# A long fused layer on one core: the closing V chunk in plain fp32, eight more gathered rows beside it, and the list work dealt anew

## The chip, the cores and the metric

One core of a Trainium2 chip runs the whole kernel in one launch. The metric is the device time of one execution in microseconds (us), as the median of the runs. The profile and the trace are of one further execution.

## The reference, cut to what matters

The kernel computes one layer of a hybrid network on 256 tokens of width 2048: retention and a gated linear recurrence side by side, cross attention, and then a layer of single-neuron experts, which is where the change lies. Everything is float32.

```python
def peer_ffn(xn, w_q, sub_keys, u_tab, v_tab):
    ...                                      # scores over 2 x 128 sub-keys, 8 heads
    eid = (i1 * PEER_N_KEYS + i2)...         # 8 x 16 of 16384 experts for each token
    gate = jax.nn.softmax(top_sc, axis=-1)...
    def block(args):
        xb, eb, gb = args
        u = u_tab[eb]
        act = jax.nn.gelu(jnp.einsum('td,tkd->tk', xb, u))
        return jnp.einsum('tk,tkd->td', gb * act, v_tab[eb])
```

For each token, 128 experts are chosen; each adds gate * gelu(u . x) * v to the token's row. A final RMSNorm over the row follows.

## The kernel before, in words

**Two ways to an expert.** The 16384 experts lie in 128 groups of 128. Some groups are done for all tokens as dense matrix products: 40 fixed ones (chunks 0 to 4 of eight groups each, tables U and V in a layout of their own) and 32 that are picked at run time as the fullest (chunks 5 to 8, whose columns are gathered by indirect DMA from the tables Us and Vs). What is left of each token's choices is done row by row: this is the *list*. For each half of the tokens (tt 0 and 1; 128 tokens lie on the 128 partitions) and each of 38 slots k (BASE), one indirect DMA gathers a row of Us for every token (128 rows of 8 KB), a *dot* (line 1438, VectorE) multiplies it with x and sums; later one gathers the row of Vs and an *axpy* (line 1446, VectorE) adds it, scaled, to the result hh. Two more gathers, the *spill*, hold what did not fit; their rows enter by TensorE (lines 1643, 1665).

**Stages.** `steps` is a list of steps made by `u_steps` and `v_steps` and run by `run`. First come the U products of chunks 5 to 8 (64 steps: a gathered column is transposed on TensorE, split and multiplied). Then come the V products in the order of ORDER: chunks 0, 1, 2, 3, 5, 6, 7, 8, with 16 steps each, into eight PSUM tiles `acc`. The ninth, chunk 4, is the closing one and is written out in `v_final`.

**Two forms of a V step.** A rounded step splits its table tile into `hi` (a cast to fp32r, ScalarE, line 1364) and `lo` (the rest, VectorE, line 1383) and its activations likewise, and issues three fp32r products: hi with both activation parts, lo with the first (lines 1175 to 1178 in `v_mms`, 1188 to 1191 in `r_mms`). A plain step, for the chunks named in PLAIN (5 and 7), multiplies the float32 tile as it stands (line 1197 in `p_mms`), with no hi and lo. The activations of a chunk that is not plain are split by `rounded` and `left` (lines 1307 and 1311), attached to the steps of the chunk before.

**Who deals the list.** The list is a generator, `chosen`. After each step, `run` calls `wv.pump(step.rate)`: it adds the step's rate to a credit and lets the list run while there is credit; a list item costs 2.2. The rates are RU for U steps on gathered columns, RV for rounded V steps, RP for plain ones. Each item first issues the gathers for which a buffer of `ring` is free (on POOL's queue, line 1431), then its own dot or axpy. All instructions of an engine run in the order written; so a rate decides how many dots, axpys and gathers stand between two steps on VectorE and POOL. What is left when the steps have run out is drained.

**The closing chunk.** END takes the last list axpys out of the list; `ending` deals them out one to a tile of the closing chunk, with three buffers in turn. Between the steps and the closing chunk stands a branch that is not taken with these data (line 1556, `rest`, more rows for tokens that overflow); every engine passes it. `v_final` loads its 16 V tiles on SP's queue (line 126) into four raw buffers, splits each (`high`, `low`), and multiplies it by `v_mms`. Tiles of output quarter 3 are kept split and come last, once for each tt, so that the first half of the tokens can be normed and written while the second is multiplied.

```python
RG, RK, RU, RV, RP = 8.0, 3.5, 1.9, 1.25, 3.1
PLAIN = (5, 7)
END = 4
ORDER = (0, 1, 2, 3, 5, 6, 7, 8, 4)
```

## Time and profile before

| | us |
|---|---|
| median of 3 runs | 2041.74 (2039.88 to 2043.61) |
| the profiled execution, its own time | 2037.77 |
| its span | 2036.0 |
| TensorE busy (a busy TensorE is not one at its peak) | 1895.3 |
| VectorE busy | 1539.9 |
| ScalarE busy | 882.8 |
| POOL busy | 520.8 |

Times of the trace are microseconds from the span's start. The U steps on gathered columns run from about 1278 to 1508 us, V chunks 0 to 3 to 1723, chunk 5 (plain) and chunk 6 to 1848, chunk 7 (plain) and chunk 8 to 1976, the closing chunk and the norm to 2036. PE stands for TensorE, PEld for its weight loads, DVE for VectorE, ACT for ScalarE, SP for SyncE. One plain float32 matmul leaves two MATMUL records in the trace.

### The profile page before, as it was taken

How to read it: one execution, taken by the hardware profiler on the slowest of the kernel's cores; microseconds unless marked ns; L12 is line 12 of the kernel's file. 1: busy time of each engine (PE TensorE's matmuls, PEld its weight loads, DVE VectorE, ACT ScalarE, POOL GpSimd, SP SyncE). 2: the span in 40 equal slices, each digit the busy share in tenths (PEclk: the TensorE clock that was granted, in tenths of full speed). 3: DMA queues.
4: the chain of work that ended last, by engine and by line, in shares of the span. 5: the costliest groups of instructions: out<-in, count | busy, mean ns of one | idle time of the engine just before them, and what ended most of it. 6: DMA issues, size and time to landing. Idle time of an engine off the chain costs nothing.

```text
span 2036.0 us, 27487 instructions
## 1 busy us (share of the span) xinstructions
PE 1895.3 (93%) x10068; PEld 1574.0 (77%) x10068; DVE 1539.9 (76%) x2366; ACT 882.8 (43%) x1382; POOL 520.8 (26%) x371
## 2 busy tenths in 40 slices
PE   9999999999999999999889778999998998969698
PEld 8888888888889888888788667899886776455376
DVE  6868967754566557999967666999797987776866
ACT  6556444544555555554456523333343432020143
POOL 1200010000000000000055410555434566765621
PEclk9999999999999999999999889999999998989899
DMA  8775656566555467556458685998989899989963
GB/s 293 264 219 171 200 177 197 160 191 192 186 176 156 145 185 288 169 178 201 155 131 172 160 274 183 394 385 291 381 320 410 290 348 378 366 310 398 362 241 123
DMA packets 203244, 499.86 MB, mean 246 GB/s; under 512 B 106760, under 2 KB 113032, under 8 KB 174856
## 3 DMA queue, kind: packets, MB, share of 16 engines
q1 hardware_dynamic: 72288, 254.23, 38.1%
q0 software_dynamic: 36240, 228.29, 29.1%
q10 hardware_dynamic: 94576, 15.54, 4.4%
q8 instruction: 79, 1.29, 0.3%
q14 instruction: 61, 0.50, 0.1%
HBM read 503.24 MB, written 21.30 MB: 258 GB/s over the span
## 4 chain that ended last, share of the span: by engine, by line
PE 51%; DMA 15%; issue 12%; DVE 12%; POOL 6%; ACT 2%; ACTq 1%; POOLq 0%; SPq 0%; DVEq 0%
PE wb L143 10%; PE xc L186 6%; PE xc L185 6%; PE xc L188 6%; PE wb L145 5%; DMA at<-in_Us_dram,idx 4%; DMA at<-in_Vs_dram,idx 3%; DVE lo L134 3%; POOL at L1431 3%; PE U L143 3%; PE U L145 1%; DMA h<-in_Vs_dram,idx 1%; PE G L1127 1%; DMA gt<-gs 1%; PE acc L1178 1%
## 5 line engine op out<-in xcount | busy, mean ns | idle before, releaser
L134 DVE TENSOR_TENSOR lo<-raw,hi 128x1024 fp32r<-128x1024 f32 x364 | 448.9, 1235 | 207.3 <-PE xc L188 125.6
L133 ACT CAST hi<-raw 128x1024 fp32r<-128x1024 f32 x364 | 381.7, 1051 | 290.0 <-PE xc L186 175.2
L143 PE MATMUL U<-xn,hi 128*128 128x512 f32 x1152 | 310.9, 406 | 0.0
L143 PEld LDWEIGHTS U<-xn,hi 128*128 128x128 f32 x1152 | 211.6, 194 | 36.1 <-ACT hi L133 0.2
L1438 DVE SCALAR_TENSOR_TENSOR junk<-at,h 128x2048 bf16<-128x2048 f32 x71 | 162.3, 2286 | 19.3 <-DMA at<-in_Us_dram,idx 19.3
L145 PEld LDWEIGHTS U<-xn,lo 128*128 128x128 f32 x1152 | 157.6, 192 | 23.6 <-DVE lo L134 12.7
L145 PE MATMUL U<-xn,lo 128*128 128x256 f32 x1152 | 163.2, 285 | 9.7 <-DVE lo L134 9.7
L1446 DVE SCALAR_TENSOR_TENSOR hh<-at,coef,hh 128x2048 f32<-128x2048 f32 x54 | 127.0, 2351 | 45.4 <-DMA at<-in_Vs_dram,idx 43.8
L1364 ACT CAST hi<-kept 128x1024 fp32r<-128x1024 f32 x52 | 53.6, 1050 | 220.5 <-DMA kept<-in_Vs_dram,dyn 138.2
L781 POOL DMA_DIRECT2D hn<-h x2 | 1.1, 564 | 509.6 <-DVE h L779 509.6
L1431 POOL DMA_INDIRECT at<-in_Us_dram,idx x71 | 83.9, 1181 | 132.4 <-DVE junk L1438 100.9
L143 PE MATMUL wb<-hT,hi 128*128 128x512 f32 x448 | 116.9, 397 | 0.0
L1197 PE MATMUL acc<-kept,kept 128*128 128x512 f32 x256 | 111.0, 594 | 3.0 <-DMA kept<-in_Vs_dram,dyn 3.0
L1431 POOL DMA_INDIRECT at<-in_Vs_dram,idx x54 | 100.1, 1854 | 48.9 <-DVE hh L1446 26.9
L1114 POOL TENSOR_TENSOR kept<-kept 128x512 f32<-128x512 bf16 x64 | 77.7, 1222 | 122.3 <-DVE kept L1113 89.3
L1175 PE MATMUL acc<-hi,xe 128*128 128x512 f32 x240 | 97.4, 406 | 6.6 <-ACT hi L1364 6.6
L1197 PEld LDWEIGHTS acc<-kept,kept 128*128 128x128 f32 x256 | 48.5, 190 | 64.4 <-issue 58.5
L1176 PE MATMUL acc<-hi,xe 128*128 128x512 f32 x240 | 95.9, 400 | 0.0
L1113 DVE TENSOR_TENSOR kept<-kept,kept 128x512 bf16<-128x512 bf16 x128 | 70.0, 595 | 28.4 <-POOL kept L1114 17.3
L143 PEld LDWEIGHTS wb<-hT,hi 128*128 128x128 f32 x448 | 80.7, 189 | 13.9
L1127 PE MATMUL G<-kept,kept 128*128 128x128 f32 x512 | 73.8, 296 | 18.6 <-POOL kept L1114 10.2
L143 PE MATMUL wb<-xT,hi 128*128 128x512 f32 x352 | 89.8, 397 | 0.0
(500 smaller groups left out, 4150.2 us busy)
## 6 DMA issues: line engine op xcount, KB each, us to landing
raw<-in_U_dram SPq DMA_DIRECT2D x80, 512.0 KB, 4.0
raw<-in_V_dram SPq DMA_DIRECT2D x60, 512.0 KB, 6.4
raw<-in_w_qkv_dram SPq DMA_DIRECT2D x48, 512.0 KB, 3.6
raw<-in_w_xyg_dram SPq DMA_DIRECT2D x44, 512.0 KB, 4.3
raw<-in_w_xk_dram SPq DMA_DIRECT2D x32, 512.0 KB, 3.5
raw<-in_w_xv_dram SPq DMA_DIRECT2D x32, 512.0 KB, 3.6
raw<-in_w_out_dram SPq DMA_DIRECT2D x32, 512.0 KB, 3.5
raw<-in_w_xq_dram SPq DMA_DIRECT2D x32, 512.0 KB, 3.5
```

The lines of the kernel that those rows point to most:

```text
L133: A.copy(hi, raw)
L134: V.tensor_tensor(lo, raw, hi.bitcast(F32), op=ALU.subtract)
L143: PE.matmul(pt, hi[:, ks], xt[:, kb, :], start=(kb == 0), stop=(kb == KB - 1))
L145: PE.matmul(pt[:, :T], lo[:, ks], xt[:, kb, :T], start=False, stop=False)
L185: PE.matmul(pt, xh, hi[:, w], start=(n == 0 and k == 0), stop=False)
L186: PE.matmul(pt, xl, hi[:, w], start=False, stop=False)
L188: PE.matmul(pt, xh, lo[:, w], start=False, stop=(n == 7 and k == 1))
L1175: PE.matmul(pt, ah[:, c, t_], hi[:, w], start=(first and c == 0), stop=False)
L1197: PE.matmul(acc[dc][tt], av[:, c, tt * P:(tt + 1) * P], row[:, dc * 512:(dc + 1) * 512], start=False, stop=False)
L1431: G.indirect_dma_start(dst, None, src, bass.IndirectOffsetOnAxis(ap=ix, axis=0), bounds_check=n - 1, oob_is_err=False)
L1438: V.scalar_tensor_tensor(junk, gat, 1.0, h[0], op0=ALU.mult, op1=ALU.mult, accum_out=coef[tt][:, k:k + 1])
L1446: V.scalar_tensor_tensor(hh[tt], gat, coef[tt][:, k:k + 1], hh[tt], op0=ALU.mult, op1=ALU.add)
```

## The change

Three edits go together.

1. Chunk 4 joins PLAIN. It is the closing one, so `v_steps` still makes no plain steps for it (a chunk under NCH keeps its form), but its activations are no longer split, and `v_final` multiplies float32 tiles as they are loaded: no `high`, no `low`, four plain matmuls a tile in place of twelve fp32r ones. Its tiles go into the buffers of raw, hi and lo in turn, eleven in all, ten loaded ahead.
2. END goes from 4 to 12: eight more axpys leave the list for the closing chunk. `ending` uses all free buffers, five, in place of three.
3. The rates are set anew: RU 1.9 to 2.05, RV 1.25 to 1.2, RP 3.1 to 2.0.

`dot` takes a first slot k0, which matters only behind the branch.

```diff
-RG, RK, RU, RV, RP = 8.0, 3.5, 1.9, 1.25, 3.1
-PLAIN = (5, 7)
-END = 4
+RG, RK, RU, RV, RP = 8.0, 3.5, 2.05, 1.2, 2.0
+PLAIN = (4, 5, 7)
+END = 12
...
-        if i in PLAIN:
+        if i in PLAIN and i >= NCH:
...
     def ending():
         free = ring + [h[0]]
+        deep = len(free) - 1
         held = []
-        for m in range(len(closing) + 3):
-            if m >= 3:
-                _, tt, k, _ = closing[m - 3]
-                axpy(tt, k, held[m - 3])
+        for m in range(len(closing) + deep):
             if m < len(closing):
                 _, tt, k, _ = closing[m]
-                held.append(fetch(free[m % 3], a["Vs"], NS, idx[tt][:, k:k + 1]))
-            if m >= 2:
+                held.append(fetch(free[m % len(free)], a["Vs"], NS, idx[tt][:, k:k + 1]))
+            if m >= deep:
+                _, tt, k, _ = closing[m - deep]
+                axpy(tt, k, held[m - deep])
                 yield
...
         def load(t):
             if t < len(tiles):
                 dc, q = tiles[t]
-                raws[t] = raw_tile(a["V"][i, dc, q])
+                tag, n = (("raw", 4), ("hi", 4), ("lo", 3))[(0, 1, 0, 1, 2, 0, 1, 2, 0, 1, 2)[t % 11]]
+                raws[t] = ws.tile([P, 1024], F32, tag=tag, name="last", bufs=n)
+                nc.sync.dma_start(raws[t], a["V"][i, dc, q])
...
+        def products(t, tts):
+            dc, q = tiles[t]
+            for tt in tts:
+                for k in range(2):
+                    c = 2 * q + k
+                    PE.matmul(acc[dc][tt], av[:, c, tt * P:(tt + 1) * P], raws[t][:, k * 512:(k + 1) * 512],
+                              start=False, stop=False)
...
-                v_mms(ah, al, his[t], los[t], q, list(enumerate(acc[dc])))
+                products(t, range(TT))
...
-                if t in (0, 2) or t > 2:
-                    next(last_rows, None)
+                next(last_rows, None)
...
-                v_mms(ah, al, vl[q][:, 0], vl[q][:, 1], q, [(tt, pt)])
+                products(12 + q, (tt,))
```

The list's rows (dots, spill dots and axpys on VectorE), counted in the two written orders: U stage 54 before and 58 now; V chunks 0 to 3 together 37 and 36; chunk 5 21 and 14; chunk 6 10 and 9; chunk 7 21 and 14; chunk 8 7 and 11; closing 4 and 12.

Gathers on POOL's queue in chunk 7. L1263 is a column of the chunk, 1 MB for two steps; L1431 a row of the list, 1 MB too; the names are the buffers. Before:

```order
L1263 DMA kept_7753<-in_Vs_dram,dyn 128x2048
L1431 DMA at_10570<-in_Vs_dram,idx 128x2048
L1431 DMA at_10566<-in_Vs_dram,idx 128x2048
L1263 DMA kept_7747<-in_Vs_dram,dyn 128x2048
L1431 DMA h_4236<-in_Vs_dram,idx 128x2048
L1431 DMA at_10568<-in_Vs_dram,idx 128x2048
L1431 DMA at_10570<-in_Vs_dram,idx 128x2048
L1263 DMA kept_7748<-in_Vs_dram,dyn 128x2048
L1431 DMA at_10566<-in_Vs_dram,idx 128x2048
L1431 DMA h_4236<-in_Vs_dram,idx 128x2048
L1431 DMA at_10568<-in_Vs_dram,idx 128x2048
L1263 DMA kept_7752<-in_Vs_dram,dyn 128x2048
```

Now:

```order
L1263 DMA kept_7753<-in_Vs_dram,dyn 128x2048
L1431 DMA at_10568<-in_Vs_dram,idx 128x2048
L1431 DMA h_4236<-in_Vs_dram,idx 128x2048
L1263 DMA kept_7747<-in_Vs_dram,dyn 128x2048
L1431 DMA at_10570<-in_Vs_dram,idx 128x2048
L1431 DMA at_10566<-in_Vs_dram,idx 128x2048
L1263 DMA kept_7748<-in_Vs_dram,dyn 128x2048
L1431 DMA at_10568<-in_Vs_dram,idx 128x2048
L1431 DMA h_4236<-in_Vs_dram,idx 128x2048
L1263 DMA kept_7752<-in_Vs_dram,dyn 128x2048
```

Where three list rows stood between two columns for most of the chunk, there are two now.

VectorE at the end of chunk 8, up to the branch (L1555 loads its condition). L1383 is a lo of chunk 8, L1446 an axpy, L1288 a gate of chunk 4, L1524 and L1528 the weights of the spill. Before:

```order
L1446 SCALAR_TENSOR_TENSOR hh_14527<-at_10568,coef,hh_14527 128x2048
L1288 TENSOR_TENSOR kept_7755<-raw,kept_7755 128x8x128
L1383 TENSOR_TENSOR lo<-kept_7747,hi 128x1024
L1446 SCALAR_TENSOR_TENSOR hh_14527<-kept_7749,coef,hh_14527 128x2048
L1383 TENSOR_TENSOR lo<-kept_7747,hi 128x1024
L1383 TENSOR_TENSOR lo<-kept_7752,hi 128x1024 x2
L1524 TENSOR_TENSOR od<-od,spg 128x2
L1528 TENSOR_SCALAR oh<-iota,spt,od 128x128 x2
L1383 TENSOR_TENSOR lo<-kept_7748,hi 128x1024
L1555 TENSOR_LOAD many
L1556 COMPARE_AND_BRANCH
```

Now:

```order
L1383 TENSOR_TENSOR lo<-kept_7748,hi 128x1024
L1383 TENSOR_TENSOR lo<-kept_7751,hi 128x1024
L1446 SCALAR_TENSOR_TENSOR hh_14543<-at_10570,coef,hh_14543 128x2048
L1383 TENSOR_TENSOR lo<-kept_7751,hi 128x1024
L1383 TENSOR_TENSOR lo<-kept_7754,hi 128x1024
L1446 SCALAR_TENSOR_TENSOR hh_14543<-at_10566,coef,hh_14543 128x2048
L1383 TENSOR_TENSOR lo<-kept_7754,hi 128x1024
L1446 SCALAR_TENSOR_TENSOR hh_14543<-at_10568,coef,hh_14543 128x2048
L1446 SCALAR_TENSOR_TENSOR hh_14543<-h_4236,coef,hh_14543 128x2048
L1555 TENSOR_LOAD many
L1556 COMPARE_AND_BRANCH
```

Before, the list ended in the middle of chunk 8 and the branch stood ahead of the last five lo's; now list rows are dealt up to the last lo and two stand behind it, and the branch stands behind these.

VectorE in the closing chunk as it is now, behind the branch. L1619 adds a finished output quarter:

```order
L1556 UNCONDITIONAL_BRANCH x2
L1446 SCALAR_TENSOR_TENSOR hh_14543<-at_10568,coef,hh_14543 128x2048
L1446 SCALAR_TENSOR_TENSOR hh_14543<-h_4236,coef,hh_14543 128x2048
L1446 SCALAR_TENSOR_TENSOR hh_14543<-kept_7749,coef,hh_14543 128x2048
L1446 SCALAR_TENSOR_TENSOR hh_14543<-kept_7750,coef,hh_14543 128x2048
L1446 SCALAR_TENSOR_TENSOR hh_14543<-h_4235,coef,hh_14543 128x2048
L1619 TENSOR_TENSOR hh_14542<-hh_14542,acc_14196 128x512
```

Five axpys from five buffers stand ahead of the first quarter's sum; before, the 16 lo's of the closing chunk stood here with four axpys among them.

## Rows read from the trace of the kernel before

**Rows 1.** The page's head and its part 1: busy us (share of the span) and instructions of TensorE.

```profile
span 2036.0 us, 27487 instructions
PE 1895.3 (93%) x10068; PEld 1574.0 (77%) x10068; DVE 1539.9 (76%) x2366; ACT 882.8 (43%) x1382; POOL 520.8 (26%) x371
```

**Rows 2.** Busy time by stage: the stretch and its us, then busy us and instructions of PE, PEld, DVE, ACT and POOL, the granted clock, the DMA share, GB/s of recorded packets.

```profile
1278.00:1508.00 230.00, 225.32 (x1447) 202.01 (x1447) 204.73 (x267) 85.73 (x186) 112.13 (x83) 0.99 0.92 351
1508.00:1723.00 215.00, 187.54 (x771) 149.10 (x770) 179.71 (x149) 72.88 (x76) 122.70 (x75) 0.94 0.94 359
1723.00:1848.00 125.00, 105.90 (x321) 62.99 (x320) 93.13 (x49) 18.30 (x18) 89.89 (x50) 0.93 0.90 344
1848.00:1976.00 128.00, 105.74 (x322) 64.28 (x321) 91.51 (x54) 26.15 (x27) 67.41 (x40) 0.91 0.87 335
1976.00:2036.00 60.00, 50.85 (x210) 38.97 (x208) 36.79 (x48) 21.59 (x34) 9.67 (x7) 0.95 0.39 134
```

**Rows 3.** What TensorE waited for from 1508 to 1976 us: us in total, times, the longest.

```profile
PE acc L1191 <- DVE lo L1383: 33.5, 9, 15.5
PE acc L1178 <- DVE lo L1383: 19.4, 9, 9.2
```

**Rows 4.** What VectorE waited for from 1640 to 1950 us, the longest in total.

```profile
DVE hh L1446 <- DMA at<-in_Vs_dram,idx: 43.8, 23, 7.7
```

**Rows 5.** DMA issues from 1278 to 1425 us (U stage): number, median us from issue to landing. All gathers of 1.05 MB.

```profile
at<-in_Us_dram,idx POOLq DMA_INDIRECT x34, 8.6
row<-in_Us_dram,dyn POOLq DMA_INDIRECT x14, 9.4
h<-in_Us_dram,dyn POOLq DMA_INDIRECT x7, 9.7
at<-in_Us_dram,spi POOLq DMA_INDIRECT x1, 6.2
```

**Rows 6.** The same from 1723 to 1930 us (chunks 5, 6, 7 and the start of 8), with the line on recorded packets.

```profile
DMA packets 11283, 74.06 MB, mean 358 GB/s; under 512 B 2247, under 2 KB 2247, under 8 KB 2247
...
at<-in_Vs_dram,idx POOLq DMA_INDIRECT x39, 9.4
kept<-in_Vs_dram,dyn POOLq DMA_INDIRECT x26, 8.8
h<-in_Vs_dram,idx POOLq DMA_INDIRECT x14, 9.6
```

**Rows 7.** The same over the whole U stage, 1278 to 1508 us. Where a size stands (KB each), it is that; the rest are gathers of 1.05 MB.

```profile
h<-hn POOLq DMA_DIRECT2D x1, 1024.0 KB, 7.6
at<-in_Us_dram,idx POOLq DMA_INDIRECT x51, 8.2
raw<-in_V_dram SPq DMA_DIRECT2D x1, 512.0 KB, 3.9
row<-in_Us_dram,dyn POOLq DMA_INDIRECT x18, 9.5
h<-in_Us_dram,dyn POOLq DMA_INDIRECT x9, 9.7
at<-in_Us_dram,spi POOLq DMA_INDIRECT x2, 8.3
at<-hn,spti POOLq DMA_INDIRECT x2, 7.6
```

**Rows 8.** The same over chunks 5 to 8, 1723 to 1976 us.

```profile
raw<-in_V_dram SPq DMA_DIRECT2D x6, 512.0 KB, 6.8
fg<-in_fg_dram SPq DMA_DIRECT2D x1, 1024.0 KB, 7.5
at<-in_Vs_dram,idx POOLq DMA_INDIRECT x41, 9.3
kept<-in_Vs_dram,dyn POOLq DMA_INDIRECT x29, 8.8
h<-in_Vs_dram,idx POOLq DMA_INDIRECT x15, 9.6
kept<-in_Vs_dram,idx POOLq DMA_INDIRECT x2, 7.1
at<-in_Vs_dram,spi POOLq DMA_INDIRECT x2, 14.8
```

**Rows 9.** TensorE's timeline at the first and behind the last matmul of chunk 7, plain: start, us, then the line and the operation.

```profile
1848.26 2.74 PE L1197 MATMUL acc<-kept,kept 128*128 128x512 f32 x6
...
1902.79 0.79 PE L1188 MATMUL acc<-hi,xe 128*128 128x512 f32 x1
```

**Rows 10.** TensorE's timeline at the first matmul of the closing chunk and behind its fourth tile, where the spill rows enter.

```profile
1976.11 0.39 PE L1175 MATMUL acc<-hi,xe 128*128 128x512 f32 x1
...
1986.99 1.88 PE L1643 MATMUL acc<-at,oh 128*128 128x512 f32 x4
```

**Rows 11.** From part 5 of the page, the axpy: number, busy us, mean ns of one, idle time of VectorE ahead of them and what ended it.

```profile
L1446 DVE SCALAR_TENSOR_TENSOR hh<-at,coef,hh 128x2048 f32<-128x2048 f32 x54 | 127.0, 2351 | 45.4 <-DMA at<-in_Vs_dram,idx 43.8
```

**Rows 12.** The timelines of VectorE and of POOL at the branch: start, us, and in brackets the idle time before and what ended it.

```profile
1960.51 1.23 DVE L1383 TENSOR_TENSOR lo<-kept,hi 128x1024 fp32r<-128x1024 f32 x1 [3.15 <-DVEq L1556]
1962.13 1.61 POOL L1431 DMA_INDIRECT h<-in_Vs_dram,idx  x1 [16.64 <-DVE lo L1383]
```

**Rows 13.** The line on recorded packets from 1508 to 1723 us (chunks 0 to 3).

```profile
DMA packets 17248, 77.24 MB, mean 359 GB/s; under 512 B 3092, under 2 KB 3092, under 8 KB 12564
```

More of the change, by code (lines that the diff above doesn't have):

```diff
@@ L1435, in hybrid_layer_kernel, with dot @@
     coef = {}
-    def dot(tt, k, gat, last):
+    def dot(tt, k, gat, last, k0=0):
         V.scalar_tensor_tensor(junk, gat, 1.0, h[0], op0=ALU.mult, op1=ALU.mult, accum_out=coef[tt][:, k:k + 1])
         if k % 8 == 7 or k == last:
-            s = slice(k - k % 8, k + 1)
+            s = slice(max(k - k % 8, k0), k + 1)
             A.activation(coef[tt][:, s], coef[tt][:, s], AF.Gelu_apprx_tanh)
@@ L1560, in rows_more @@
                 hold(tt)
-                for f, tab in ((lambda k, g: dot(tt, k, g, k0 + n - 1), "Us"), (lambda k, g: axpy(tt, k, g), "Vs")):
+                for f, tab in ((lambda k, g: dot(tt, k, g, k0 + n - 1, k0), "Us"), (lambda k, g: axpy(tt, k, g), "Vs")):
                     for k in range(k0, k0 + n):
@@ L1595, in square @@
             A.activation(j, hh[tt][:, ds], AF.Square, accum_out=ss3[:, tt, dc:dc + 1])
-        ah, al = ahs.pop(i)
-        vl = [tp.tile([P, 2, 1024], F32R, tag="act", name="vl", bufs=NCH + NDY) for q in range(4)]
+        av = acts[i]
         tiles = [(dc, q) for dc in range(4) for q in range(4)]
-        raws, his, los = {}, {}, {}
+        raws = {}
         def load(t):
@@ L1604, in load @@
                 dc, q = tiles[t]
-                raws[t] = raw_tile(a["V"][i, dc, q])
-        def high(t):
-            if t < len(tiles):
-                dc, q = tiles[t]
-                his[t] = vl[q][:, 0] if dc == 3 else ws.tile([P, 1024], F32R, tag="hi", name="hi", bufs=4)
-                A.copy(his[t], raws[t])
-        def low(t):
-            if t < len(tiles):
-                dc, q = tiles[t]
-                los[t] = vl[q][:, 1] if dc == 3 else ws.tile([P, 1024], F32R, tag="lo", name="lo", bufs=3)
-                V.tensor_tensor(los[t], raws[t], his[t].bitcast(F32), op=ALU.subtract)
+                tag, n = (("raw", 4), ("hi", 4), ("lo", 3))[(0, 1, 0, 1, 2, 0, 1, 2, 0, 1, 2)[t % 11]]
[8 more added lines that the diff above has]
+                              start=False, stop=False)
         def added(dc):
@@ L1624, in v_final @@
         with tc.manual_schedule(engines=ENGINES):
-            for t in range(4):
+            for t in range(10):
                 load(t)
-            for t in range(3):
-                high(t)
-            for t in range(2):
-                low(t)
-                load(t + 4)
             last_rows = ending()
@@ L1634, in v_final @@
                 dc, q = tiles[t]
-                high(t + 3)
-                low(t + 2)
-                load(t + 6)
+                load(t + 10)
                 if q == 1 and dc:
                     added(dc - 1)
-                v_mms(ah, al, his[t], los[t], q, list(enumerate(acc[dc])))
+                products(t, range(TT))
                 if q == 3:
@@ L1644, in v_final @@
                                   start=False, stop=True)
-                if t in (0, 2) or t > 2:
-                    next(last_rows, None)
-            for t in range(12, 16):
-                high(t + 3)
-                low(t + 2)
+                next(last_rows, None)
             for _ in last_rows:
```

## The prediction

> **What bounds the kernel now.** I read the page first: TensorE is busy 1895 of 2036 us [rows 1]. A mean over such different stages says little, so I cut the part of the program that the change reaches into its stages [rows 2]: U stage on gathered columns (1278 to 1508 us), V chunks 0 to 3 (to 1723), the pair plain chunk 5 and rounded chunk 6 (to 1848), the pair plain 7 and rounded 8 (to 1976), and the closing chunk 4. TensorE is busy for 225 of 230 us in the first and for 51 of 60 in the last; in between it stands idle for 27, 19 and 22 us. The DMA share is 0.87 to 0.94 in the first four stages and 0.39 in the last. So the closing chunk has bandwidth to give away and the stages ahead of it have not.
>
> Who stops TensorE there? The waits say VectorE: 33.5 us before a lo of line 1383 in chunks 6 and 8, 19.4 us in chunks 0 to 3 [rows 3]. But VectorE itself waits, in order, for gathered rows: 43.8 us before the axpy of line 1446 for rows in the at buffers alone [rows 4]. A lo that stands behind an axpy waits with it. So the limit is the gathers.
>
> How fast can they come? The megabytes in a DMA row are those of recorded packets; I count issues instead, since a row gather is 128 x 2048 x 4 bytes = 1.05 MB. From 1278 to 1425 us there are 56 of them, 58.7 MB in 147 us, **0.399 MB per us** [rows 5]; there TensorE runs without a gap worth naming. From 1723 to 1930 us it is 79, 82.8 MB in 207 us, **0.400** [rows 6]. Two stages with different engines at the same rate: I take 0.400 as what the DMA gives. Over whole stages, stalls included, the counts are 87.6 MB in 230 us (0.381) [rows 7] and 97.5 MB in 253 us (0.385) [rows 8]. These are my bounds below. Above, I use TensorE's own time.
>
> **The change, part by part.** The listed orders count the list's rows by stage. U stage: 54 before, 58 now. V chunks 0 to 3: 37 and 36. Plain 5: 21 and 14. Rounded 6: 10 and 9. Plain 7: 21 and 14. Rounded 8: 7 and 11. Closing: 4 and 12.
>
> *U stage, +6.6 us.* Four more rows. In the gap-free stretch 35 of the 56 gathers are list rows; 58/54 of them are 37.6, together 61.4 MB, at 0.400 153.6 us instead of 147. The rest of the stage (1425 to 1508) has slack, because POOL waits there for the new h. Ends: 0, if the engines carry 0.418 (the DMA share of 0.92 leaves that open), and +11, if the stage keeps its own mean: 91.8 MB at 0.381 are 241 us, now 230. I take the middle because the stretch of [rows 5] is the nearest row.
>
> *Chunks 0 to 3, -2.6 us.* One row less, 1.05 MB at 0.400. Ends 0 and -2.6. The waits for gt rows at the gates stay.
>
> *Chunks 5 to 8, -38 us.* Eleven rows fewer: 97.5 - 11.5 = 86.0 MB, at 0.400 215 us instead of 253. Ends: at the stages' own 0.385 it is 223, so -30; TensorE's floor is the other end. A plain chunk takes 1848.26 to 1902.79, 54.5 us [rows 9]. A rounded one takes 16 x 2.72 = 43.5 us (four tiles of the closing chunk from 1976.11 to 1986.99 [rows 10]). Two of each are 196 us, so -57. Between the ends I stay at the counted rate, since the plain chunks are now asked for (14 + 8) x 1.05 MB = 23.1 MB in 54.5 us, 0.423: still a little above it, where before 29 rows and columns, 30.4 MB, asked for 0.558. In chunk 8 the list now lasts to the end; the free last eight steps of before (1953 to 1976, no gap) are lost, and that is inside these bytes.
>
> *Closing chunk, +11.0 us.* TensorE is the bound there. 16 tiles of 12 fp32r matmuls, 43.5 us [rows 10], become 64 plain matmuls, which by chunk 7 take 54.5 us [rows 9]. Ends 11 and 11: same operand shapes, clock 0.95 and more in both. The spill matmuls (L1643, L1665) stay.
>
> *The eight extra closing rows, +2 us.* Their 8 x 2.35 us on VectorE [rows 11] fit into a 60 us stage with 16 lo's taken out (16 x 1.23 us [rows 12]), so VectorE costs nothing; the cover is TensorE, and if it were gone the eight would cost 19 us; POOL, busy 9.7 of 60 us [rows 2], takes eight issues of 1 to 2 us. What can be late is the transfer. The fetches wait for VectorE to pass the branch of line 1556; before, VectorE is past it at 1960.51 and the first fetch follows at 1962.13 [rows 12], 14 us ahead of the stage. Now it stands behind the last two list axpys, some 3 us after chunk 8's end (the branch itself costs VectorE 3.15 us [rows 12]). From there 12 rows, up to 16 V tiles and 2 spill rows are at most 23 MB: 58 us at 0.400, while TensorE needs 61. So 0 at one end; at 0.381 they are 60.6 us, the last axpy ends near +66 us and the final scaling of the first half, 5 us of short VectorE work ahead of the second, comes late: +11 at the other. I take 2, because most tiles are loaded before the stage begins: eleven buffers stand ready, of which seven are freed by chunk 8's last four steps.
>
> *Free.* The rounding of chunk 4's activations (two casts, two subtractions of 1.2 us) and the closing casts on ACT, an engine with 26 busy of 128 us [rows 2]; if it were full, the 16 casts would cost 17 us. On SP the tile loads keep their place behind fg; those into hi buffers wait for TensorE instead of VectorE, and what is queued behind them is only the next tile. The dealing of coef slices (line 1440) changes only code that the data does not reach.
>
> **Sum.** +6.6 - 2.6 - 38 + 11.0 + 2 = -21.0 us against the profiled execution of 2037.77 us (span 2036.0), that is 2016.8. The median of the runs is 2041.74, 4 us higher; on it the forecast is **2021 us**.
>
> **The rivals.**
>
> *Chunks 5 to 8 reach TensorE's floor, 1994 us.* If plain stages no longer pile up a backlog, the long waits of 15.5 and 9.2 us [rows 3] go, and with them the lowered clock of 0.93 and 0.91 [rows 2]: 0 - 2.6 - 57 + 11 + 0 = -48.6 with no cost in the U stage; on the median 1993 to 1994. For it: demand falls to about the rate. Against: chunks 0 to 3 ask for no more than that today and idle 27 of 215 us [rows 2].
>
> *The closing rows come late, 2030 us.* The terms above with +11 in place of +2: -12. For it: the fetch now stands behind the list's last axpys. Against: the stage's DMA share is 0.39 [rows 2].
>
> *The rate falls, slower, 2048 us.* One mechanism, in all three stages: with rows and tiles evenly spread there is no slack, both queues are always in flight, and the DMA yields 0.381, the U stage's whole mean, everywhere. U +11; chunks 0 to 3: 77.24 MB recorded [rows 13], scaled by 82.8/74.06 [rows 6], are an estimated 86.4 MB, less one row 85.3, at 0.381 224 us instead of 215, +9; chunks 5 to 8: 226 instead of 253, -27; closing +13: together +6, on the median 2048. It decides from the rate at which 91.8 + 85.3 + 86.0 MB take 230 + 215 + 253 - 13 = 685 us, 0.384. For it: whole stages show 0.381 and 0.385. Against: those means hold stretches in which POOL waited or the list had run out, and the two full stretches show 0.399 and 0.400.
>
> The Trainium skill, "DMA: Bandwidth & Descriptors", section "Where 436 GB/s comes from", says that for transfers from HBM the memory's share per core, about 358 GB/s, binds. By that figure the same 263.1 MB would take 735 us and the time would be an estimated 2092. The counted rates of this case, 399 and 400, disagree with it, so it gets 2 of the slower rival's 13 parts in a hundred.
>
> **How the numbers follow.** Chances: forecast 0.50 (its own range 2010 to 2034), floor 0.14, late closing rows 0.15, rate 0.13; the 0.08 left lie between late rows and falling rate, within 0.2%. 0.2% is 4 us, about what a measurement of this kernel can tell from no change. So faster 0.79, same 0.08, slower 0.13. The range leaves out the floor's lower half and the rate's upper part: **2002 to 2041**.
>
> **What would show it.** Right: TensorE idle from 1723's counterpart to the closing chunk down from 41 us to about 20; the plain chunks at 54 to 58 us with the next rounded chunk starting at once, and no wait of 15 us before a lo; a U stage longer by 4 to 9 us with rows waited for; a closing chunk of 61 to 64 us at a DMA share above 0.7. Wrong: a U stage lengthened by over 11 us; gaps of over 5 us between chunks 6 and 8; VectorE reaching its last axpy after TensorE's last dc 2 tile. If chunks 5 to 8 lose under 20 us, it was not the bytes that held them, and the forecast's main term is wrong.

## The result and the profile after

| | us |
|---|---|
| before, median of 6 runs | 2040.01 (2037.16 to 2043.61) |
| changed, median of 6 runs | 2028.73 (2025.13 to 2036.53) |
| ratio | 0.9948, 95% interval 0.9929 to 0.9968 |
| changed, profiled execution | 2025.13, span 2023.3 (before 2037.77 and 2036.0) |
| changed, again beside the last experiments, median of 6 | 2023.87 (2019.65 to 2029.61), ratio 0.9918, 0.9896 to 0.9939 |

The change makes the kernel faster by about 11 us, or 15 in the second measurement. The forecast was 2021 in a range of 2002 to 2041. The direction and the range held; the gain was about half to three quarters of the 21 us forecast. Runs of one kernel differ by 5 us and more to either side, so a single profile says where time goes and the medians say how much.

The stages of the changed kernel, cut at its own boundaries; columns as in [rows 2], which they answer:

```profile
1278.00:1514.00 236.00, 227.59 (x1439) 201.72 (x1438) 210.91 (x272) 87.53 (x190) 116.71 (x86) 0.98 0.92 356
1514.00:1729.00 215.00, 186.97 (x771) 149.94 (x771) 178.48 (x145) 72.50 (x76) 123.14 (x74) 0.94 0.93 356
1729.00:1837.00 108.00, 100.14 (x322) 60.22 (x321) 73.11 (x41) 18.71 (x19) 63.97 (x39) 1.00 0.84 314
1837.00:1952.00 115.00, 100.80 (x318) 60.97 (x317) 79.34 (x45) 17.24 (x17) 57.39 (x37) 0.94 0.91 365
1952.00:2023.00 71.00, 62.20 (x146) 27.35 (x144) 40.72 (x42) 8.70 (x21) 26.26 (x18) 0.96 0.54 208
```

The U stage is 6 us longer, chunks 0 to 3 as long as before, chunk 5 with 6 18 us shorter, chunk 7 with 8 12 us shorter, the closing chunk with the norm 11 us longer. The DMA share in the third stretch fell from 0.90 to 0.84 and TensorE still has gaps of 8 and 14 us in the third and fourth: neither is full.

What TensorE waited for from 1508 to 1976 us, against [rows 3]:

```profile
PE acc L1178 <- DVE lo L1383: 23.1, 9, 6.0
PE acc L1191 <- DVE lo L1383: 18.7, 6, 11.8
```

The wait in the rounded chunks 6 and 8 went from 33.5 to 18.7 us; two thirds of what is left is one wait of 11.8 us. The plain chunk 7 itself, against [rows 9], on TensorE's timeline:

```profile
1836.36 55.09 PE L1197 MATMUL acc<-kept,kept 128*128 128x512 f32 x128
1890.89 0.79 PE L1188 MATMUL acc<-hi,xe 128*128 128x512 f32 x1
```

It takes 54.5 us, as before, and chunk 8 starts at once. So the wait is inside chunk 8. Three timelines around it. First TensorE:

```profile
1924.72 2.08 PE L1191 MATMUL acc<-lo,xe 128*128 128x512 f32 x4 [11.77 <-DVE lo L1383]
1926.59 0.63 PE L1188 MATMUL acc<-hi,xe 128*128 128x512 f32 x1
...
1929.09 0.39 PE L1188 MATMUL acc<-hi,xe 128*128 128x512 f32 x1
```

VectorE over the same time:

```profile
1921.18 2.35 DVE L1446 SCALAR_TENSOR_TENSOR hh<-h,coef,hh 128x2048 f32<-128x2048 f32 x1 [10.41 <-DMA h<-in_Vs_dram,idx]
1923.44 3.49 DVE L1383 TENSOR_TENSOR lo<-kept,hi 128x1024 fp32r<-128x1024 f32 x3
```

POOL, which issues that row:

```profile
1896.78 2.85 POOL L1263 DMA_INDIRECT kept<-in_Vs_dram,dyn  x1 [5.51 <-DVE lo L1383]
1899.94 1.97 POOL L1431 DMA_INDIRECT at<-in_Vs_dram,idx  x1 [0.30 <-issue]
1902.21 1.96 POOL L1263 DMA_INDIRECT kept<-in_Vs_dram,dyn  x1 [0.31 <-issue]
1904.47 1.97 POOL L1263 DMA_INDIRECT kept<-in_Vs_dram,dyn  x1 [0.30 <-issue]
1906.75 0.99 POOL L1431 DMA_INDIRECT h<-in_Vs_dram,idx  x1 [0.30 <-issue]
```

Read from the bottom up. Three lo's of TensorE's next steps stand behind one axpy. That axpy waits 10.4 us for a row issued at 1906.75 and there at 1921.2, 14.4 us later. The row was issued late because POOL's queue had stood for 5.5 us (1891.3 to 1896.8) before a column whose buffer a lo had yet to read; the gathers behind it then followed at 0.3 us from each other, so their buffers had been free. Three columns went out ahead of the row. So the DMA, full a moment before, had almost nothing to do, and then everything at once. In the 25 us from 1896 the slices of recorded DMA traffic go like this (each 0.63 us):

```profile
GB/s 433 419 249 105 26 26 79 197 210 380 419 419 393 419 406 433 380 367 393 380 210 249 419 380 380 406 433 419 419 419 446 406 419 439 413 439 400 426 439 420
```

This is a hold-up of order, not a lack of bandwidth: some 3 us of the DMA's time are lost, and the row that VectorE needs comes behind them. I had not predicted it. It is one of four such waits on POOL of 4 us and more in chunks 5 to 8; x1 below has their sum. The closing chunk, TensorE, against [rows 10]:

```profile
1952.24 13.89 PE L1613 MATMUL acc<-last,kept 128*128 128x512 f32 x32
...
2005.46 1.02 PE L1651 MATMUL acc<-at,oh 128*128 128x512 f32 x2
...
2013.18 1.02 PE L1651 MATMUL acc<-at,oh 128*128 128x512 f32 x2
```

TensorE runs through it without a wait, 62.0 us against 50.8. VectorE's first and last closing axpy and the first sum that needs TensorE's end:

```profile
1966.51 2.35 DVE L1446 SCALAR_TENSOR_TENSOR hh<-at,coef,hh 128x2048 f32<-128x2048 f32 x1 [15.61 <-DMA at<-in_Vs_dram,idx]
...
2001.00 2.35 DVE L1446 SCALAR_TENSOR_TENSOR hh<-h,coef,hh 128x2048 f32<-128x2048 f32 x1
...
2006.52 0.69 DVE L1652 TENSOR_TENSOR hh<-hh,acc 128x512 f32<-128x512 f32 x1 [1.97 <-PE acc L1651]
```

The twelve rows are done at 2003.4, and VectorE still waits 2 us for TensorE: they cost nothing, with 2 us to spare.

### The profile page after: what moved, and what is told of

Read it like the earlier page. It is cut to its first block, busy times and chain, and to the rows that moved or that the text cites. A ratio compares the mean times of both kernels' runs of the same rounds, so it can differ in the third digit from the quotient of the medians.

```text
span 2023.3 us, 27282 instructions
## 1 busy us (share of the span) xinstructions
PE 1897.9 (94%) x10004; PEld 1556.1 (77%) x10004; DVE 1518.9 (75%) x2348; ACT 863.6 (43%) x1364; POOL 508.4 (25%) x371
## 3 DMA queue, kind: packets, MB, share of 16 engines
q0 software_dynamic: 36240, 228.29, 29.0%
## 4 chain that ended last, share of the span: by engine, by line
PE 55%; DMA 15%; DVE 11%; issue 10%; POOL 5%; ACT 2%; ACTq 1%; POOLq 0%; SPq 0%; DVEq 0%
PE wb L143 10%; PE xc L185 6%; PE xc L186 6%; PE xc L188 6%; PE wb L145 5%; PE U L143 5%; DMA at<-in_Us_dram,idx 4%; PE acc L1613 3%; DVE lo L134 3%; PE U L145 2%; DMA gt<-gs 2%; DMA raw<-in_V_dram 2%; POOL at L1431 2%; DMA kept<-in_Vs_dram,dyn 1%; PE G L1127 1%
## 5 line engine op out<-in xcount | busy, mean ns | idle before, releaser
L1446 DVE SCALAR_TENSOR_TENSOR hh<-at,coef,hh 128x2048 f32<-128x2048 f32 x49 | 116.0, 2368 | 50.1 <-DMA at<-in_Vs_dram,idx 49.4
L1431 POOL DMA_INDIRECT at<-in_Us_dram,idx x72 | 82.4, 1144 | 125.2 <-DVE junk L1438 102.0
L1431 POOL DMA_INDIRECT at<-in_Vs_dram,idx x49 | 73.4, 1498 | 66.3 <-DVE hh L1446 28.8
L1127 PEld LDWEIGHTS G<-kept,kept 128*128 128x128 f32 x512 | 67.2, 207 | 22.4 <-POOL kept L1114 13.1
L1380 DVE TENSOR_TENSOR lo<-uT,hi 128x512 fp32r<-128x512 f32 x128 | 82.0, 684 | 2.4 <-ACT hi L1362 1.4
```

Source lines behind the costliest of these rows:

```text
L1127: PE.matmul(pt.rearrange("p (c t) -> p c t", t=4)[:, :, j], o1[:, j], og[:, j], start=True, stop=True)
L1431: G.indirect_dma_start(dst, None, src, bass.IndirectOffsetOnAxis(ap=ix, axis=0), bounds_check=n - 1, oob_is_err=False)
L1446: V.scalar_tensor_tensor(hh[tt], gat, coef[tt][:, k:k + 1], hh[tt], op0=ALU.mult, op1=ALU.add)
```

## The experiments

The theory after the result was that hold-ups in the order of the queues (H), not the mean rate of the gathers as in the forecast (F), set what is left in chunks 5 to 8. Each kernel's edit stands against the one it is made from. In the expectations, list items are counted where a step deals them; the written order on VectorE differs from that by one or two. All stage lengths below are from one profiled execution each, in us (a stage begins with TensorE's first product of it); the column behind them runs from the closing chunk's first product to the end of the span.

| kernel | U ends at | chunks 0 to 3 | chunks 5 to 8 | closing, norm | median (ratio to before, 95%) |
|---|---|---|---|---|---|
| before | 1508.2 | 214.9 | 253.0 | 59.9 | 2040.0 |
| changed | 1514.2 | 214.6 | 223.5 | 71.1 | 2028.7 (0.9929 to 0.9968) |
| changed, again | 1515.9 | 220.6 | 220.2 | 71.1 | 2023.9 (0.9896 to 0.9939) |
| e1 rates only | 1515.8 | 218.4 | 223.2 | 81.2 | 2035.7 (0.9964 to 0.9996) |
| e2 END 4 | 1516.5 | 220.4 | 220.7 | 79.6 | 2036.7 (0.9951 to 0.9988) |
| e3 old rates | 1508.8 | 218.9 | 237.1 | 71.1 | 2036.1 (0.9970 to 1.0002) |
| e4 rounded closing | 1513.8 | 218.6 | 220.0 | 74.0 | 2031.6 (0.9943 to 0.9978) |
| x1 late hand-back | 1516.8 | 220.8 | 203.6 | 71.1 | 2008.5 (0.9815 to 0.9853) |
| x4 and one column a step | 1513.2 | 207.2 | 201.1 | 71.1 | 2000.1 (0.9793 to 0.9827) |
| x2 no list gathers | 1511.3 | 219.0 | 196.9 | 71.1 | 2000.1 (one run) |
| x3 no list axpys | 1516.4 | 214.5 | 196.9 | 71.1 | 2000.8 (one run) |
| y1 before, with x4's edits | 1507.0 | 212.3 | 249.7 | 59.9 | 2029.6 (0.9928 to 0.9966) |
| y3 x4, rounded closing | 1517.4 | 208.2 | 200.2 | 78.7 | 2006.3 (0.9820 to 0.9867) |
| y4 x4, old rates | 1505.3 | 210.9 | 235.8 | 71.0 | 2031.9 (0.9941 to 0.9975) |

### The three edits of the change, one at a time (e1 to e4)

**e1**, the kernel before with the new rates:

```diff
-RG, RK, RU, RV, RP = 8.0, 3.5, 1.9, 1.25, 3.1
+RG, RK, RU, RV, RP = 8.0, 3.5, 2.05, 1.2, 2.0
```

> The kernel before with the three new rates alone (2.05, 1.2, 2.0); four closing rows and the rounded closing chunk stay. Up to the end of chunk 8 the list is dealt as in the changed kernel, so 8 rows are left over, and they are drained between the last lo of chunk 8 and the branch. Theory (the gain comes from taking 8 rows out of chunks 5 to 8 and giving them to a closing chunk that does not wait for VectorE): chunk 8 ends some 24 us earlier than before, as in the changed kernel, and the drained rows, 8 x 2.6 us, and the branch then hold up the closing lo's by about as much: 2036 to 2042 us, no gain. Rival (dealing the list more evenly is enough, the closing form is beside the point): the 24 us stay, 2016 to 2022 us.

Measured 2035.7, just below the expected band and far from the rival. Chunks 5 to 8 shrink to 223 us, as in the changed kernel. The eight rows left over then stand on VectorE ahead of the closing lo's, and TensorE's timeline shows the price in one row:

```profile
1978.32 2.08 PE L1178 MATMUL acc<-lo,xe 128*128 128x512 f32 x4 [18.93 <-DVE lo L1617]
```

The rates make the gain; without END it is given back at the closing chunk.

**e2**, the changed kernel with END back:

```diff
-END = 12
+END = 4
```

> The changed kernel with END set back to 4: plain closing chunk, new rates, and 8 rows drained after chunk 8 instead of dealt into the closing chunk. TensorE's closing products need nothing of VectorE, but the two spill rows are fetched only when the list is done, so their matmuls at the end of the first output quarter stand still. Theory: spill rows land some 20 us later than in the changed kernel, 1952 + 8 x 2.6 + about 9, while TensorE comes to them at 1966: plus 15 to 20 us, 2044 to 2049. Rival (the plain form alone frees the closing chunk, END only names the rows): 2027 to 2031, as the changed kernel.

Measured 2036.7: between the two. TensorE does wait for a spill row, but for 6.4 us and not 15 to 20: on POOL's timeline all but two of the list's rows are issued by 1957.5, when chunk 8 ends, and the two spill rows follow at 1964.7 and 1967.1:

```profile
1978.02 3.75 PE L1633 MATMUL acc<-at,oh 128*128 128x512 f32 x4 [6.44 <-DMA at<-in_Vs_dram,idx]
```

The closing stage is 8.5 us longer. END is worth that much even beside a plain closing chunk, for the spill's sake.

**e3**, the changed kernel with the old rates (e1's diff turned round):

> The changed kernel with the old rates (1.9, 1.25, 3.1); END 12 and the plain closing chunk stay. The list's items by 16 steps: U 56 instead of 60, then 9, 9, 9, 9, and 23, 9, 18 and 0 in chunks 5 to 8 instead of 15, 8, 15 and 9. Theory by bytes alone (a mean rate holds chunks 5 to 8): three rows more there, plus 8 us, U stage minus 6.8 us: 2028 to 2032, no difference. Rival (a stretch dealt above the rate makes a backlog that the next rounded chunk pays for with its own wait): chunks 5 and 6 as before, 125 us, chunk 7 57 us, chunk 8 free of the list at 46 us: 228 us against 223.5, so 2026 to 2028 with the 15 us wait in chunk 6 back in the trace. The two are near in time; the trace tells them apart by the waits.

Measured 2036.1, slower than both expected. Chunks 5 and 6 take 125.1 us as before; chunk 7 and 8 take 112.0 although chunk 8 has no list rows. TensorE waits 7.6 us for a lo in chunk 6, where 15 were expected, and 11.6 at the start of chunk 8, where none was. That is the pattern of the kernel before, whose 15.5 us wait lies at the start of chunk 8 and not in chunk 6, as I had placed it:

```profile
1823.07 2.07 PE L1191 MATMUL acc<-lo,xe 128*128 128x512 f32 x4 [7.64 <-DVE lo L1383]
...
1920.69 2.08 PE L1191 MATMUL acc<-lo,xe 128*128 128x512 f32 x4 [15.52 <-DVE lo L1383]
```

Three rows more cost 14 to 17 us, not 8: so it isn't a matter of the sum of bytes. y4 below tells why.

**e4**, the changed kernel with the rounded closing chunk of before, twelve rows beside it:

```diff
-                products(t, range(TT))
+                high(t + 3)
+                low(t + 2)
...
+                v_mms(ah, al, his[t], los[t], q, list(enumerate(acc[dc])))
```

> The changed kernel (12 closing rows, five buffers, new rates) with the closing chunk rounded as before. TensorE needs 11 us less there. Theory (the rows land from 14 us after the chunk's start and stand between the lo's on VectorE, so TensorE waits for lo's behind late rows): the last axpy stays at about 2001 to 2003, three lo's and the products of the last quarter follow, plus 0 to 6 us on the changed kernel: 2028 to 2035. Rival (VectorE has room, 12 x 2.35 + 16 x 1.22 + 8 x 0.65 = 53 us in a 62 us stretch, so the shorter rounded products win): 2016 to 2020.

Measured 2031.6, in the theory's band. TensorE is busy 53.7 us there instead of 62, but the stage is 3 us longer (74.0 against 71.1). On VectorE's timeline the last axpy, now among 16 lo's, ends 57.4 us after the closing chunk's start, against 51.1 in the changed kernel:

```profile
2007.53 2.34 DVE L1446 SCALAR_TENSOR_TENSOR hh<-h,coef,hh 128x2048 f32<-128x2048 f32 x1
```

So the plain form earns about 3 us in the stage by clearing VectorE, not TensorE. It is the smallest part of the change; by the medians alone it is not clear of the noise (the intervals of the table overlap).

### Bytes, VectorE's work, or order (x2, x3, x1, x4)

**x2**, the changed kernel without the list's gathers from the 99th on:

```diff
-                held.append(fetch(ring.pop(0), src, n, ix))
+                held.append(ring.pop(0) if taken >= 98 else fetch(ring.pop(0), src, n, ix))
```

> The changed kernel with the list's gathers from the 99th on (the Vs rows of chunks 5 to 8) left out: their axpys stay and work on what the buffers hold, the columns' gathers and the closing rows stay. Theories F and H (the transfers, by rate or by order, hold the stage): chunks 5 to 8 at TensorE's own 196 to 202 us instead of 223.5, 1998 to 2006 us. Rival V (VectorE's own work, 47 axpys of 2.35 us among the lo's, holds it): 215 to 224 us, 2020 to 2029.

**x3**, all gathers, but not the list's axpys from the 19th on:

```diff
-                axpy(tt, k, mine[0])
+                n_axpy[0] += 1
+                if n_axpy[0] <= 18:
+                    axpy(tt, k, mine[0])
```

> The changed kernel with the list's axpys from the 19th on left out: all gathers stay, those of the list's rows too, but VectorE does not wait for them. Theory F (rate): the columns queue among the same 84 MB, at 0.40 MB per us 210 us or more, chunks 5 to 8 at 210 to 220 us, 2013 to 2025 us. Theory H (hold-up in VectorE's order): TensorE waits for nothing but a column now and then, 196 to 205 us, 1998 to 2009 us.

Both, one execution each, ran chunks 5 to 8 in 196.9 us, TensorE without a gap. The row of x2 and then that of x3, columns as in [rows 2]:

```profile
1730.40:1927.30 196.90, 196.90 (x642) 120.70 (x641) 152.91 (x85) 36.15 (x35) 56.09 (x31) 1.00 0.51 181
```

```profile
1731.10:1928.00 196.90, 196.90 (x641) 120.69 (x640) 47.75 (x39) 36.16 (x35) 83.29 (x75) 1.00 0.96 384
```

x2 keeps VectorE's work (152.9 us busy) and drops the transfers; x3 keeps the transfers and drops the work. Each alone fits into TensorE's time. In x3 the DMA issues are those of the changed kernel:

```profile
last<-in_V_dram SPq DMA_DIRECT2D x10, 512.0 KB
fg<-in_fg_dram SPq DMA_DIRECT2D x1, 1024.0 KB
at<-in_Vs_dram,idx POOLq DMA_INDIRECT x31
kept<-in_Vs_dram,dyn POOLq DMA_INDIRECT x29
h<-in_Vs_dram,idx POOLq DMA_INDIRECT x11
kept<-in_Vs_dram,idx POOLq DMA_INDIRECT x2
at<-in_Vs_dram,spi POOLq DMA_INDIRECT x2
```

75 gathers of 1.05 MB, ten tiles of 0.52 and fg are, in the forecast's own count, 84.9 MB in 196.9 us: **0.431 MB per us**. So F's 0.400 was no ceiling. Together the two runs leave the coupling: an axpy in VectorE's order that waits for a row issued too late.

The count itself is too high, for the forecast and for the figures of 0.426 in the expectations. In the changed kernel two spill gathers are alone on POOL's queue between 1938 and 1957.5 us, and the twelve closing rows between 1957.5 and 1997. Packets, MB and share of that queue, first for the two, then for the twelve:

```profile
q0 software_dynamic: 288, 2.10, 29.9%
```

```profile
q0 software_dynamic: 1728, 5.99, 39.9%
```

A spill gather moved 1.05 MB, a closing row 0.50. Where a token has no expert left for a slot, `rows_of` gives the slot an index beyond the table and `fetch` has a bounds check: by the code such rows are left out (I did not read the indices themselves). x2 leaves out 46 list gathers, and its trace holds 41.6 MB less on that queue than the changed kernel's (186.72 against 228.29): 0.90 MB each. So recorded packets, not issues, tell what the DMA moved. Its pace when full shows in the second half of x3's stretch:

```profile
1830.00:1928.00 98.00, 98.00 (x320) 60.14 (x320) 23.08 (x19) 17.29 (x17) 34.64 (x33) 1.00 1.00 411
```

That is 0.411 MB per us at a DMA share of 1.00. The stretches from which the forecast took its 0.400 moved 354 and 358 GB/s.

**x1**, the changed kernel; a rounded step hands its buffer back when its products are written:

```diff
             elif kind == "R" and steps[t].part:
-                rows_v.append(raws[t])
+                split[t] = raws[t]
...
                 step.mms(his.pop(t), los.pop(t))
+                if t in split:
+                    rows_v.append(split.pop(t))
```

> The changed kernel, with one edit: in a rounded V step the column's buffer is handed back when the step's products are written, as in a plain step, not two steps earlier with its lo. So at the start of a rounded chunk the next column's gather no longer stands at the head of POOL's queue waiting for a lo that VectorE has not reached (5.5 us at 1891 to 1897 in the changed kernel, in which nothing is issued), and the gathers do not come in a burst after it. Theory H (hold-ups: the queue stands, the DMA runs empty, a burst of columns delays a row, and lo's wait behind the axpy that waits for it): the 11.8 us wait before a lo in chunk 8 goes to 3 or less and chunks 7 and 8 take 104 to 108 us instead of 115: 2017 to 2023 us. Theory F (the forecast's: the gathers' mean rate of 0.40 MB per us sets the length of chunks 5 to 8): the same bytes in the same time, 2026 to 2031.

Measured **2008.5**, more than H expected. No instruction is added or dropped and the same bytes move; only the place of the columns in POOL's queue changes. TensorE's waits in chunks 5 to 8, where the changed kernel has 18.7 and 11.8:

```profile
PE acc L1191 <- DVE lo L1383: 3.7, 3, 2.5
```

And POOL's waits there, ahead of a column, for a lo; first the changed kernel, then x1:

```profile
POOL kept L1263 <- DVE lo L1383: 23.9, 6, 7.3
```

```profile
POOL kept L1263 <- DVE lo L1383: 1.2, 4, 0.3
```

The standstill is gone, and chunks 5 to 8 are 17 to 20 us shorter than in the two profiles of the changed kernel.

**x4**, x1 and at most one column's gather a step, once the steps run:

```diff
+                c0 = len(q)
-                while q and q[0] <= t + (4 if k == "R" else 0) and free[k]:
+                while q and q[0] <= t + (4 if k == "R" else 0) and free[k] and (k != "R" or t < 9 or len(q) == c0):
```

> As the run before, and each step issues at most one column's gather, so that columns and list rows alternate on POOL's queue where three or four columns stood in a row. Theory H: no wait above 4 us before a lo in chunks 6 and 8, chunks 5 to 8 at 203 to 212 us, 2012 to 2020 us. Theory F: no change, 2026 to 2031.

Measured **2000.1**, below H's band, and the best of all versions: 1.9% under the kernel before. The row of chunks 5 and 6, then of 7 and 8:

```profile
1720.50:1820.40 99.90, 99.70 (x322) 60.01 (x321) 76.20 (x42) 18.35 (x18) 75.65 (x40) 1.00 0.95 364
1820.40:1921.60 101.20, 99.36 (x322) 60.11 (x321) 78.53 (x44) 17.52 (x17) 63.83 (x35) 1.00 1.01 418
```

TensorE is busy in all but 2 of 201 us at a granted clock of 1.00. Against x1's profile chunks 5 to 8 gain 2.5 us; 13.5 more lie in chunks 0 to 3, where three columns of chunk 5 used to go out together. The four profiles with one column a step show 207 to 212 us there, the ten others of this table 214 to 221; how that comes about I did not isolate.

### The hold-ups without the change, and the change again (y1, y3, y4)

**y1**, the kernel before with x4's edits and nothing else:

> The kernel before with the two edits of the run x4 (a rounded step's buffer handed back with its products; one column a step), nothing of the change. Theory H (hold-ups in the order of the queues, not the rate, cost chunks 5 to 8 their time; the DMA gives 0.426 MB per us as in the run without axpys, 84 MB in 197 us): chunks 5 to 8 move 97.5 MB in 229 us instead of 253, chunks 0 to 3 gain 0 to 8: 2008 to 2018 us, more than the whole change gained. Theory F (0.40 MB per us is the limit): 244 us or more in chunks 5 to 8, 2028 to 2035.

Measured 2029.6: H's number is missed, and F's band holds the time, though x3 rules out its reason. Chunks 5 to 8 shrink from 253 to 249.7 only, with a 17.5 us wait before a lo at the start of chunk 8:

```profile
1915.19 2.07 PE L1191 MATMUL acc<-lo,xe 128*128 128x512 f32 x4 [17.53 <-DVE lo L1384]
```

Here bytes do bind, but locally: in chunk 7, ahead of that wait, the DMA is full from end to end, with TensorE busy throughout:

```profile
1841.00:1895.00 54.00, 54.00 (x127) 23.97 (x126) 35.90 (x16) 2.90 (x3) 33.48 (x20) 1.00 1.01 414
```

In chunks 5 and 6, 122 us, it moves 360 GB/s, with a hole between the two; there it isn't full throughout.

**The changed kernel again:**

> The changed kernel itself, unedited, beside the other runs on this chip: 2025 to 2034 us by its own spread. Its trace is a second execution: U stage at 234 to 238 us, chunks 0 to 3 at 214 to 221, chunks 5 to 8 at 220 to 225, a wait of over 8 us before a lo in chunk 8 if that wait is of the order and not of chance.

Measured 2023.9, a little under the band. The same standstill is there on POOL, and behind it TensorE waits 10.5 us for a lo at 1918 to 1929:

```profile
1902.06 2.86 POOL L1263 DMA_INDIRECT kept<-in_Vs_dram,dyn  x1 [5.52 <-DVE lo L1383]
```

**y3**, x4 with e4's rounded closing chunk:

> The run x4 with the closing chunk rounded as before (12 closing rows stay): is the plain form worth anything once the hold-ups are gone? Theory (the closing rows land late, so VectorE, not TensorE, sets the end, in either form): 2000 to 2007 us, 0 to 6 above x4. Rival (11 us less of TensorE come through): 1988 to 1994.

Measured 2006.3, in the theory's band: the closing stage takes 78.7 us against 71.1. The plain form is worth 6 us here by the medians.

**y4**, x4 with the old rates:

> The run x4 with the old rates (1.9, 1.25, 3.1), closing chunk plain with 12 rows: 56 list items in the U stage instead of 60, 50 in chunks 5 to 8 instead of 47, 41 of them in the first three. Theory H: U stage minus 6.6, chunks 5 to 7 carry 24 columns and 41 rows, 68 MB in 160 us at 0.426 where TensorE needs 152, chunk 8 is free of the list: plus 5 to 10 in chunks 5 to 8, so 1997 to 2004 us, no difference from x4. Rival (uneven dealing costs by itself, as it did without the edits, where the old rates were 7 us slower than the new): 2005 to 2010.

Measured 2031.9: H missed, and the rival was nearer, though too low by over 20 us. Chunks 5 to 8 take 235.8 us, as in e3 without the edits. TensorE's timeline at the start of chunk 8, and VectorE's:

```profile
1893.65 0.79 PE L1188 MATMUL acc<-hi,xe 128*128 128x512 f32 x1
...
1908.69 2.08 PE L1191 MATMUL acc<-lo,xe 128*128 128x512 f32 x4 [12.65 <-DVE lo L1384]
```

```profile
1904.44 2.35 DVE L1449 SCALAR_TENSOR_TENSOR hh<-at,coef,hh 128x2048 f32<-128x2048 f32 x1 [0.47 <-DMA at<-in_Vs_dram,idx]
...
1907.41 2.35 DVE L1384 TENSOR_TENSOR lo<-kept,hi 128x1024 fp32r<-128x1024 f32 x2
```

TensorE starts chunk 8 at 1893.7; VectorE works off the axpys dealt beside chunk 7 until 1906.8, and only then comes to the first lo. That is a backlog. A plain chunk takes 54.5 us, in which a full DMA at 0.411 MB per us moves an estimated 22.4 MB. The new rates deal it eight columns and fourteen rows (the counts of the written orders), at 1.05 and a mean of 0.90 MB an estimated 21.0 MB; the old ones eight and 21, 27.3 MB. With these chunk 5 itself runs longer, 62.8 us before and 69.2 here, because its columns queue among the rows. What a plain chunk is asked for beyond the 22.4 is paid at the start of the next rounded chunk, since TensorE needs nothing of VectorE in the plain one. So there are two mechanisms, and H alone was too little: the even deal removes the backlog, x1's and x4's edits the standstill of the queue. With the old rates the edits bring about 4 us over e3; with the new ones 24 to 29 over the changed kernel.

## Why the prediction was right, and where it wasn't

- **Direction and range: right.** Sum -21 forecast; -12.7 between the two profiles, -11.3 and -15.3 between the medians.
- **U stage, +6.6: the size right, the mechanism not shown.** +6.0 and +7.7 in the two profiles of the change. Over all profiles, the ten with RU 2.05 end the stage at 1511.3 to 1517.4, the four with 1.9 at 1505.3 to 1508.8. But I had laid the time into the stretch to 1425 us, as one that the gathers pace, and called the rest slack. In that stretch TensorE is busy from end to end:

```profile
1278.00:1425.00 147.00, 146.96 (x957) 132.14 (x957) 135.51 (x178) 55.21 (x123) 80.46 (x56) 1.00 0.93 354
```

  So TensorE sets the pace there, and the rate counted in it is what was asked for. TensorE's waits in the whole stage, before and then now, lie almost all from 1424 on, the long ones at the two dots of the spill:

```profile
PE uT L1353 <- DVE lo L1380: 4.6, 2, 3.8
```

```profile
PE uT L1353 <- DVE lo L1380: 8.0, 5, 5.0
```

  That the four rows brought these waits is not shown; the agreement in size is partly luck.
- **Chunks 0 to 3, -2.6: not shown.** -0.3 and +5.7. e3, with the old rates, has 218.9 where before has 214.9, so 4 us lie within what two executions differ by.
- **Chunks 5 to 8, -38: right sign, size off, reason half wrong.** Measured -29.5 and -32.8: the end of -30 that I had named. TensorE's idle time there fell from 41 to 22 us, as the sign of being right said. The step that failed is "I take 0.400 as what the DMA gives". Of its two stretches one was paced by TensorE (above) and the other had holes in it, and both were counted in issues at 1.05 MB, which a list row does not move. In the same count x3 reaches 0.431; in recorded packets a full DMA gives 0.411. The kernel before asked for more than that in its plain chunks and paid with a backlog: that part of the reasoning holds, with 21.0 against 27.3 MB in 54.5 us in place of 23.1 against 30.4. The new demand fits, and the floor of -57 was open. What kept 17 to 20 us of the way to it was the standstill in POOL's queue, which no step of mine had (x1); some 2 us more went with the bursts of columns (x4, one profile each), and 4 are left. That the mean of recorded packets is 340 GB/s before (85.95 MB) and after (75.90 MB) looks like a rate that holds the stage, and isn't one: x4 moves the same rows at 391. The standstill stood in the trace of before, and I had not looked there. In all of chunks 5 to 8, and then one of the seven, on POOL's timeline in chunk 6:

```profile
POOL kept L1263 <- DVE lo L1383: 20.2, 7, 8.0
```

```profile
1793.18 2.85 POOL L1263 DMA_INDIRECT kept<-in_Vs_dram,dyn  x1 [3.94 <-DVE lo L1383]
```

  After this come five columns from 1801 to 1812, an axpy that waits 7.7 us for its row, and TensorE's 7.6 us wait at 1823. The 15.5 us wait of [rows 3], in chunk 8, is the backlog.
- **"No wait of 15 us": it went, and another came.** The backlog's wait at the start of chunk 8 is gone (the longest in the first 15 us of the chunk is 1.5 us now), and the 9.2 us of chunks 0 to 3 are 6.0. But the sign that I had named for wrong, a gap of over 5 us between chunks 6 and 8, is there: the standstill's 11.8. So the main term's mechanism was not all of it, though the 30 us that chunks 5 to 8 lost are more than the 20 below which I had called the term wrong.
- **Closing chunk, +11.0: right.** 62.0 against 50.8 us of TensorE, +11.2.
- **Extra closing rows, +2: 0.** The stage is bound by TensorE with 2 us to spare. The sign "last axpy after TensorE's last dc 2 tile" came true (2003.4 against about 1997) and did no harm: it was the wrong sign, as the first half of dc 3 still runs to 2006.5. The DMA share is 0.54 and not over 0.7: the twelve rows moved 6.0 MB and not 12.6, and rows and tiles nearly all move in the first half of the stage (share 0.91 to 1985 us, 0.12 after).
- **Rivals.** Late closing rows: no, by 2 us. The falling rate: no. The floor: not reached by the change, but by x4 (201 us) and by x2 and x3 (196.9).
- The Trainium skill, "DMA: Bandwidth & Descriptors", section "Where 436 GB/s comes from", gives 358 GB/s of HBM for a core and 435 for the ports. The recorded 411 GB/s over 98 us (x3) lie above the first, so the trace disagrees with it as the limit of these gathers, and a little under the second. The 399 and 400 that the prediction held against it were counted issues; by packets those stretches moved 354 and 358.

## What to carry to other kernels

Compare demand with the rate stretch by stretch, each at its own length, and take the rate from a stretch in which the DMA is full and nothing else sets the pace; a mean over stretches with holes, or one that TensorE paces, looks like a limit and isn't one. Count what was moved, not what was issued. In a queue that runs in order, an issue whose buffer is given back by a late engine holds up all issues behind it, those with free buffers too: hand a buffer back in the program where its last reader has surely run, and mix the streams one by one. Two runs that drop the transfers and the work in turn tell rate, work and order apart at once.

## What the runs showed of the hardware

- After the wait of 11.8 us TensorE's matmul steps were 0.43 us for 4.4 us (1924.7 to 1929.1), against 0.23 before and after: the wait costs some 2 us more than its length. The granted clock is 1.00 up to 1914.9 us, some 2 us after the last matmul, 0.50 from 1916 to 1928.5, and 1.00 again from 1929.1. The Trainium skill, "TensorE: Matmul & The Clock Gate", section "Part 1: The HAM clock gate (the "warmup" mystery)", says that an idle window of about 3.4 us halves the clock and about as long a busy one restores it; the trace agrees on the halving and roughly on the times (2 to 3 us down, about 4 up).
- The standstill on POOL (5.5 us ahead of the wait in both profiles of the change) is that of a queue without overtaking. The Trainium skill, "PSUM — Partial Sum Buffer", section "Engine vs sequencer instructions", calls the queues of VectorE and GpSimd strict FIFO; the trace agrees.
- A full DMA moved 411 GB/s of recorded packets over 98 us in x3 and 414 over 54 us in y1, mostly row gathers of 8 KB rows, at DMA shares of 1.00 and 1.01.
- A gather moves fewer bytes than its shape says where its list slots are not all in use: 0.50 MB for each of the twelve closing rows, against 1.05 for a spill gather.
